# A planned instruction order: the planner's transfer rate set to 360 instead of 400 GB/s

## Chip, cores and metric

The kernel runs on one core of a Trainium2 chip. The metric is the device time of one execution in microseconds (us). A profile gives one execution in detail: its span goes from the first to the last instruction, and its own time is a little longer.

## What is computed

One layer of an encoder: 1024 tokens, width 2048, everything in float32. One input projection (2048 to 6752 columns) feeds two groups of heads, and one output projection joins them.

```python
u = x @ w_in                                    # q, k, v, z, q_idx, k_idx, w_idx, z_ssd, xbc, dt
score = sum_h relu(q_idx[h] @ k_idx.T) * w_idx[h]     # token indexer, 16 heads of 64
sel = top_k(where(chunk(key) <= chunk(query), score, -inf), 256)
o_attn = softmax(rope(q) @ rope(k)[sel].T / sqrt(128)) @ v[sel] * silu(z)   # 8 heads, 2 of k and v
o_ssd = rms_norm(ssd(silu(conv4(xbc)), dt) * silu(z_ssd)) * norm_w          # Mamba-2 mixer
out = layer_norm(2 ** 0.25 * x + concat(o_attn, o_ssd) @ w_out)
```

## The kernel before, in words

**The work.** Each float32 matrix is split into a high and a low part ("xh" and "xl" for inputs, "wh" and "wl" for weights): ACT makes the high part by a rounding copy, DVE or POOL the low part by a subtraction (`t_xst`, line 766; `w_split`, line 916). A product is then three matmuls of 128 x 128 by 128 x 512: high-high, high-low, low-high. The program is a list of pieces made by `units` (line 591). Pieces of the input projection ("T", `emit_t`, line 1163) hold one tile of 128 columns and 512 tokens each; pieces of the output projection ("O", `emit_o`, line 1213) come last. Two groups of tiles are computed as paired products, four small products in phases with sums of weights and of inputs in place of eight plain ones: first k, v and q, later the rest of xbc, zs and z. Sums of weights are made from two or three loads into the "wr" buffers (`t_wacc`, line 880); sums of inputs are made once (`t_xform`), written to scratch in HBM and read back as xfM and xfS. The output projection uses seven products in place of eight; the sums of its weights ("ts") are made long before by `t_wsum` (line 814) and stored.

**What goes on beside it.** Intermediate results go through scratch in HBM and come back: q, k, v, z, the conv outputs (c), the states of the mixer, the mixed output (mx), the halves of the paired products (p). The top-k (`t_topk`, line 1520) is a search by bits: passes of ACT with a sign and a sum, each followed by a few tiny operations on DVE. `s_q` (line 1636) stores a quarter of four heads: the target of one such store has 4 heads by 32 rows by 512. All transfers but the first few are issued by the SP queue.

**What sets the order.** The order of the instructions is not written by hand. While the program is being built, a planner (`Flow`, line 354) runs all tasks as generators beside the list of pieces. Each task says with `Need` what it waits for: free buffers, events, and the engines that it will use. When a task is let go, its instructions are put at the end of each engine's stream at once, and a model of the chip (`Sim`, line 132) moves its clocks: one for PE, DVE ("V"), ACT ("A"), POOL ("G"), the SP queue, and "D", the one lane on which all transfers follow each other. A result gets the time at which the model has it ready.

`ready` (line 432) lets a task go when these times, those of its earlier results and its events, lie before the present by the model, when buffers are free, and when the engines it names are not further ahead than `SLACK` (2600 ns; twice that for tasks of the first priority). Tasks that name "D" (`t_wsum`, `t_form`, `t_pre`, `t_gb`) are held back when the lane of the transfers is too far ahead. `pump` (line 477) lets tasks go in order of priority until the clock of PE has moved on; `await_tiles` (line 505) does so while the operands of the next matmuls are not ready by the model. `w_there` (line 961) looks at the landing of a weight before its split is placed, and `pick` (line 463) chooses DVE or POOL for some operations by the clocks.

On the chip each engine runs its stream in this order and waits by semaphores for what is really needed. The clocks of the model decide nothing there any more: if a transfer lands later than planned, the engine stands at the instruction that needs it, and so does all that is queued behind it.

**The model of a transfer** is `Sim.dma` (line 287): 350 ns of issue on the SP queue, then the bytes on the lane at a rate and 0.6 ns for each row, then `LAND`, 2500 ns, until the result may be used. A transfer also waits for one of 8 places (`lanes`) to come free.

Of the kernel before, what the change touches and what calls it, by code (L numbers as in the profile page):

```python
# [15 lines left out]
D = 2048  # L16
# [107 lines left out]
def in_dram(x):  # L124
    return "DRAM" in str(x.space)
# [6 lines left out]
class Sim:  # L132
# [154 lines left out]
    def dma(self, eng, out, in_, kw):  # L287
        q = {"SP": "SP", "A": "AQ", "G": "G"}[eng]
        lanes = self.lanes["G" if q == "G" else "H"]
        at, notes = self.deps([out], [in_], "D")  # L290
        start = max(self.clk[q], at, lanes.pop(0))
        issue = 1000.0 if eng == "G" else 350.0
        self.clk[q] = start + issue
        sb = in_ if in_dram(out) else out
        row = max(sb.ap[-1][1] * 4, 64)
        x = max(start + issue, self.clk["D"])
        self.clk["D"] = x + max(out.size(), in_.size()) * 4 * (1 / 400 + 0.6 / row)
        cell = [self.clk["D"] + self.LAND, start]
        lanes.append(cell[0])
        self.note(notes, cell, "D")  # L300
        return cell
# [1986 lines left out]
```

## Time and profile before

| what | value |
|---|---|
| runs of the kernel | 1725.16, 1729.61, 1730.37 us (median 1729.61) |
| the profiled execution, own time | 1725.14 us |
| its span | 1723.4 us |
| mean granted clock of TensorE | 0.986 |
| bytes moved by the DMA engines | 446.50 MB, 259 GB/s over the span |

How to read the profile: PE is the matmuls, PEld the loading of their stationary operand, DVE the vector engine, ACT the scalar engine, POOL the general one, SP the queue that issues transfers. A row of a timeline has the start, the duration, the engine, the line, the operation with its output and inputs by name, and in brackets how long the engine stood idle before and what ended that. A window row has the busy time and count of each engine, the granted clock (1.00 is full speed), the mean share of the 16 DMA engines that were busy, and GB/s. All instructions pass through one helper, so that they share a line and are told apart by the names of their tiles.

### The profile page before, as it was taken

To read this page: it belongs to the slowest core of one execution; us is meant where nothing else is said; L and a number is where in the kernel's file an instruction comes from. 1 tells how busy PE (TensorE), PEld (TensorE's weight loads), DVE (VectorE), ACT (ScalarE), POOL (GpSimd) and SP (SyncE) were. 2 spreads that over 40 slices of the span, in tenths; PEclk is the share of its full clock that TensorE was granted. 3 is DMA by queue.
4 is the path that set the end of the run, shared out by engine and by line. 5 is a ranking of instruction groups with operands and counts; after the bars stand their busy time and mean duration, and the time that the engine had idled before them with its cause. 6 is when DMAs were issued, how large, how long until landed. Compare 5 with 4: busy or idle time off the path is not lost. (4 is left out here: it accounts for less than half of the span.)

```text
span 1723.4 us, 24378 instructions
## 1 busy us (share of the span) xinstructions
PE 1638.7 (95%) x8044; PEld 1351.2 (78%) x8044; DVE 1353.0 (79%) x2444; ACT 1019.6 (59%) x1799; POOL 173.5 (10%) x201
## 2 busy tenths in 40 slices
PE   9999999998887989999999999989999999999997
PEld 7877788876666978778888788877888877888875
DVE  5779999787567898789996788845777677659998
ACT  5745575678666856987555478456867544532320
POOL 0000010000000000000222111222121110000110
PEclk9999999999899999999999999999999999999998
DMA  9576578988787678989666875658778999877654
GB/s 320 202 253 230 198 258 290 324 310 307 246 294 259 222 266 271 315 299 318 227 220 219 312 236 188 220 186 251 241 230 280 313 314 342 298 278 268 218 193 147
DMA packets 210215, 446.50 MB, mean 259 GB/s; under 512 B 21928, under 2 KB 61992, under 8 KB 210088
## 3 DMA queue, kind: packets, MB, share of 16 engines
q1 hardware_dynamic: 209656, 444.55, 75.9%
q8 instruction: 63, 1.03, 0.2%
q14 instruction: 64, 0.52, 0.1%
q10 hardware_dynamic: 432, 0.39, 0.1%
HBM read 338.56 MB, written 106.30 MB: 258 GB/s over the span
## 5 line engine op out<-in xcount | busy, mean ns | idle before, releaser
L313 PE MATMUL pj<-xh,wh 128*128 128x512 f32 (+1 forms) x1192 | 470.0, 394 | 25.9 <-ACT wh L313 18.0
L313 PE MATMUL pj<-xh,wl 128*128 128x512 f32 (+1 forms) x1192 | 460.1, 386 | 9.3 <-DVE wl L313 9.1
L313 PE MATMUL pj<-xl,wh 128*128 128x512 f32 (+1 forms) x1192 | 458.8, 385 | 0.1
L313 DVE TENSOR_TENSOR wl<-wr,wh 128x1024 fp32r<-128x1024 f32 (+1 forms) x179 | 213.9, 1197 | 113.2 <-ACT wh L313 112.6
L313 PEld LDWEIGHTS pj<-xh,wh 128*128 128x128 f32 x1192 | 227.1, 191 | 70.7 <-ACT wh L313 20.6
L313 PEld LDWEIGHTS pj<-xh,wl 128*128 128x128 f32 x1192 | 226.5, 190 | 58.8 <-DVE wl L313 14.4
L313 PEld LDWEIGHTS pj<-xl,wh 128*128 128x128 f32 x1192 | 227.3, 191 | 41.2 <-DVE xl L313 1.8
L313 ACT ACTIVATE wh<-wr 128x1024 fp32r<-128x1024 f32 (+1 forms) x185 | 190.6, 1033 | 106.7 <-PE pj L313 67.2
L313 PE MATMUL pj<-xh,s 128*128 128x512 f32 (+1 forms) x688 | 222.1, 385 | 1.8 <-DVE u L313 1.6
L313 PE MATMUL a<-u,u 128*128 128x512 f32 (+3 forms) x746 | 171.7, 351 | 16.4 <-DVE u L313 7.0
L313 PEld LDWEIGHTS a<-u,u 128*128 128x128 f32 x746 | 123.3, 189 | 50.1 <-DVE s L313 10.6
L313 PEld LDWEIGHTS pj<-xh,s 128*128 128x128 f32 x688 | 127.7, 188 | 27.3 <-ACT xh L313 2.3
L313 DVE TENSOR_TENSOR u<-u,u 128x512 f32<-128x512 f32 (+7 forms) x212 | 130.2, 627 | 16.1 <-DMA u<-wo 4.5
L313 ACT ACTIVATE u<-s,sm 128x768 bf16<-128x768 f32 (+7 forms) x132 | 129.6, 982 | 21.3 <-DVE sm L313 19.5
L313 DVE TENSOR_TENSOR wr<-wr,wr 128x1024 f32<-128x1024 f32 (+1 forms) x98 | 121.6, 1243 | 20.5 <-DMA wr<-wt 19.4
L313 ACT ACTIVATE u<-a 128x512 fp32r<-128x512 f32 (+4 forms) x115 | 53.4, 479 | 138.0 <-DVE u L313 66.5
L313 PE MATMUL pj<-xl,s 128*128 128x512 f32 (+1 forms) x344 | 130.8, 380 | 0.8 <-DVE xl L313 0.8
L313 ACT ACTIVATE u<-u 128x512 f32<-128x512 f32 (+4 forms) x165 | 91.9, 566 | 61.5 <-DVE u L313 57.3
L313 ACT ACTIVATE a<-a 128x512 f32<-128x512 f32 (+3 forms) x160 | 76.1, 504 | 70.3 <-PE a L313 69.2
L313 DVE TENSOR_TENSOR s<-wr,s 128x1024 fp32r<-128x1024 f32 (+2 forms) x59 | 70.8, 1200 | 30.7 <-ACT s L313 30.5
L313 DVE TENSOR_TENSOR u<-pj,u 128x512 f32<-128x512 f32 (+2 forms) x94 | 62.4, 664 | 36.7 <-PE pj L313 31.0
L313 PE MATMUL pj<-wh,xh 128*128 128x512 f32 x218 | 87.8, 403 | 1.2 <-DVE u L313 1.2
(253 smaller groups left out, 2678.9 us busy)
## 6 DMA issues: line engine op xcount, KB each, us to landing
wr<-wt SPq DMA_DIRECT2D x228, 512.0 KB, 5.3
u<-u SPq DMA_DIRECT2D x100, 256.0 KB, 5.7
u<-wo SPq DMA_DIRECT2D x79, 256.0 KB, 5.1
wr<-ts SPq DMA_DIRECT2D x32, 512.0 KB, 5.7
ts<-u SPq DMA_DIRECT2D x63, 256.0 KB, 4.3
xr<-xt SPq DMA_DIRECT2D x28, 512.0 KB, 4.9
s<-xt SPq DMA_DIRECT2D x28, 512.0 KB, 6.6
u<-mx SPq DMA_DIRECT2D x49, 256.0 KB, 6.3
```

The source lines that it names most:

```text
L313: f(*args, **kw)
```

## The change

One constant of the model: the rate at which a transfer occupies the lane. The instructions stay what they are; as the planner sees later landings, it may place them in another order.

```diff
@@ -294,7 +294,7 @@
         sb = in_ if in_dram(out) else out
         row = max(sb.ap[-1][1] * 4, 64)
         x = max(start + issue, self.clk["D"])
-        self.clk["D"] = x + max(out.size(), in_.size()) * 4 * (1 / 400 + 0.6 / row)
+        self.clk["D"] = x + max(out.size(), in_.size()) * 4 * (1 / 360 + 0.6 / row)
         cell = [self.clk["D"] + self.LAND, start]
         lanes.append(cell[0])
         self.note(notes, cell, "D")
```

## The prediction

> **What bounds the kernel now.** I read the page first, for the span and the busiest engine.
>
> ```profile
> span 1723.4 us, 24378 instructions
> PE 1638.7 (95%) x8044; PEld 1351.2 (78%) x8044; DVE 1353.0 (79%) x2444; ACT 1019.6 (59%) x1799; POOL 173.5 (10%) x201
> ```
>
> TensorE (PE) is busy for 1638.7 of 1723.4 us, so all other engines together can only move the 84.7 us in which it stands still, and whatever slower clock follows such a stop. A change of order leaves the matmuls alone, so the next question is where those 84.7 us lie. The windows view answers it by stage.
>
> ```profile
> core 0: us, PE busy (x) PEld busy (x) DVE busy (x) ACT busy (x) POOL busy (x), PEclk, DMA share, GB/s
> 400.00:650.00 250.00, 210.54 (x1084) 174.63 (x1085) 190.96 (x390) 174.86 (x310) 5.29 (x4) 0.95 0.76 265
> 425.00:463.00 38.00, 26.18 (x112) 18.82 (x111) 19.34 (x45) 22.89 (x42) 2.48 (x2) 0.89 0.74 248
> 500.00:515.00 15.00, 8.83 (x31) 6.37 (x30) 8.33 (x15) 9.89 (x19) 0.00 (x0) 0.77 0.83 296
> 545.00:570.00 25.00, 15.20 (x99) 14.20 (x98) 15.91 (x30) 16.76 (x27) 0.00 (x0) 0.80 0.64 223
> 650.00:1100.00 450.00, 444.95 (x2237) 370.71 (x2236) 369.36 (x725) 306.55 (x553) 63.53 (x66) 1.00 0.77 260
> 1100.00:1350.00 250.00, 240.83 (x1272) 201.51 (x1271) 167.78 (x339) 163.43 (x303) 46.83 (x63) 0.99 0.73 239
> 1350.00:1450.00 100.00, 96.28 (x517) 78.24 (x516) 67.60 (x122) 47.07 (x91) 10.89 (x8) 1.00 0.98 320
> 1450.00:1712.00 262.00, 257.76 (x1204) 213.22 (x1202) 217.51 (x326) 84.06 (x124) 20.88 (x16) 0.99 0.71 242
> ```
>
> Between 400 and 650 us PE loses 39.5 us (250 - 210.54), nearly half of all its idle time, at a granted clock of 0.95. The 450 us after that lose 5.1 us; from 1350 to 1450 the transfers fill the DMA engines (share 0.98) and PE still loses only 3.7 us. So the stage to look at is 400 to 650, which holds most of the first group of paired products (k, v and q). The timeline of PE has five long stops there.
>
> ```profile
> 430.97 0.79 PE L313 MATMUL pj<-xh,wh 128*128 128x512 f32 x1 [3.52 <-ACT xh L313]
> 437.45 0.69 PE L313 MATMUL pj<-xh,wh 128*128 128x512 f32 x1 [3.26 <-ACT xh L313]
> 461.46 0.80 PE L313 MATMUL pj<-xh,wl 128*128 128x512 f32 x1 [3.55 <-DVE wl L313]
> 508.30 0.80 PE L313 MATMUL pj<-xh,wh 128*128 128x512 f32 x1 [5.79 <-ACT wh L313]
> 558.74 0.58 PE L313 MATMUL pj<-xh,wh 128*128 128x256 f32 x1 [9.09 <-ACT wh L313]
> ```
>
> They add up to 25.2 us. The engine named is only the last link. The same stretches of the timeline for ACT and DVE show the link before it.
>
> ```profile
> 430.28 1.15 ACT L313 ACTIVATE xh<-xr 128x512 fp32r<-128x512 f32 x2 [1.54 <-DMA xr<-xfS]
> 457.66 1.23 DVE L313 TENSOR_TENSOR wr<-wr,wr 128x1024 f32<-128x1024 f32 x1 [3.92 <-DMA wr<-wt]
> 460.18 1.22 DVE L313 TENSOR_TENSOR wl<-wr,wh 128x1024 fp32r<-128x1024 f32 x1
> 504.88 1.15 ACT L313 ACTIVATE xh<-xr 128x512 fp32r<-128x512 f32 x2 [1.60 <-DMA xr<-xt]
> 507.21 1.04 ACT L313 ACTIVATE wh<-wr 128x1024 fp32r<-128x1024 f32 x1
> 555.34 2.41 ACT L313 ACTIVATE xh<-s 128x512 fp32r<-128x512 f32 x4 [3.89 <-DMA s<-xt]
> ```
>
> Four of the five go back to a transfer that had not landed. The one at 461.46 is the clearest: the split "wl", for which PE waits, is queued on DVE behind the sum "wr", and that sum held DVE for 3.92 us until its load arrived. The order was written as if the load would be there. (For the stop at 437.45 no row shows a transfer; ACT had been busy.) These are the places that a planned landing time can reach.
>
> After such a stop matmuls run slower for a while, which the spacing of starts shows:
>
> ```profile
> 432.29 0.63 PE L313 MATMUL pj<-xh,wl 128*128 128x512 f32 x1
> 432.71 0.63 PE L313 MATMUL pj<-xh,wh 128*128 128x512 f32 x1
> 441.73 0.39 PE L313 MATMUL pj<-xl,wh 128*128 128x512 f32 x1
> 441.96 0.39 PE L313 MATMUL pj<-xh,wl 128*128 128x512 f32 x1
> ```
>
> 0.42 us from one to the next at 432 us, 0.23 us at 442 us: half speed. A mean clock c over a window of w us is then 2(1-c)w us at half speed: 8.4 us from 425 to 463, 6.9 us from 500 to 515, 10.0 us from 545 to 570. Half of that is lost where PE was working: 4.2 us for the first three stops (1.4 each), at most 3.4 and 5.0 for the other two, since part of those may lie in the stop itself.
>
> **The change, part by part.** One constant in the planner's model of a transfer goes from 1/400 to 1/360 ns per byte. Nothing is removed or added; every cost comes through order. What the model says of a load of 512 KB in rows of 4 KB can be worked out from the code: 350 issue + 524288/400 + 0.6 x 128 + 2500 = 4.24 us before, 4.38 us after, a shift of 0.146 us; for 256 KB it is 0.073 us. In a queue of such loads the shifts add, and as a transfer also waits for one of eight places, the planned clock of SP slips with them. Against that the trace has:
>
> ```profile
> q1 hardware_dynamic: 209656, 444.55, 75.9%
> wr<-wt SPq DMA_DIRECT2D x228, 512.0 KB, 5.3
> ```
>
> First, landing: 5.3 us in the median, so the model is early by 1.06 us and the change takes back 0.146 of it, 14%. Second, rate: 444.55 MB in 75.9% of 1723.4 us are 340 GB/s while the engines work. The model's lane is busy 444.55 MB/400 = 1111 us plus 0.6 ns for each of 209656 packets (an estimate that takes a packet for a row), 126 us: 1237 us before, 1361 us after, and the measured 1308 us lie between. So the rate as a whole gets no truer, and the landing a little.
>
> What follows is a change of order only where a task's readiness lies within the shift. The planner compares a landing with its clock at each step; a shift of 0.15 us for a lone load and of one or two us in a queue of ten flips some choices, and each flip moves instructions and their transfers on SP, ACT, DVE and PE behind others. A flip is not proportional to the shift: a sum such as the one at 457.66 goes behind the split entirely or not at all. Its price is therefore that of a whole stop, its number is small.
>
> Price of the gain: nothing if no stop is hit. If all five went, 25.2 + 4.2 + 3.4 + 5.0 = 37.8 us. I take the two stops at 430.97 and 461.46, which are short, have a head-of-queue wait on a transfer behind them (1.54 and 3.92 us), and so are nearest to what a shift of one or two us can dissolve: 3.52 + 3.55 + 2 x 1.4 = 9.9 us. What is late next there is the load itself, still 1.06 us later than the old plan has it, under other work on ACT and DVE.
>
> Price of the loss: a stop of the kind at 558.74 made new elsewhere, 9.1 to 14.1 us with its slow clock; I take the middle, 11.6 us, because the share of slow time within the stop can't be read from the rows.
>
> The long stop has a cause that the constant can't reach:
>
> ```profile
> 545.10 1.04 SPq L313 DMA_DIRECT2D s<-xt  x2
> 547.23 1.98 SPq L313 DMA_DIRECT2D q<-u  x2
> ```
>
> ```profile
> L313 SPq DMA_DIRECT2D q<-u x16: 511/530/1359, 395.3 to 555.5; - x16
> ```
>
> ```profile
> DMA  9257987569697997899799865422222222255655
> GB/s 225 89 218 314 396 355 232 191 253 287 246 294 253 300 321 307 362 355 341 321 423 396 355 246 225 191 109 109 109 96 109 109 82 109 114 198 164 210 186 198
> ```
>
> (the last fence is the row of slices for 544 to 556 us, 0.3 us each). From 552 us on, the transfers move 109 GB/s at a share of 0.2, three or four engines of sixteen, while ACT waits for "s<-xt" until 555.34. All 16 stores "q<-u" of the kernel lie between 395.3 and 555.5 us, in the stage with the long stops, and a few engines are still working off something when the others are done. The planner knows one lane only. The Trainium skill, in "DMA: Bandwidth & Descriptors", section "Why a DMA increments its semaphore by 16 and not by 1", says that a transfer runs on the largest number of engines, up to 16, that divides the slowest dimensions of both its sides; that is 4 for a q store, whose target begins with 4 heads. The 109 GB/s agree with it. By that the wait at 558.74 is a matter of which transfers meet, and I leave it in the sum of the forecast.
>
> Two covers to test. The planner holds the preparation of the sums of the output weights back when its lane runs ahead of PE, and a slower lane does so oftener:
>
> ```profile
> L313 SPq DMA_DIRECT2D ts<-u x63: 319/327/1457, 88.8 to 955.3; - x63
> L313 SPq DMA_DIRECT2D wr<-ts x32: 319/320/587, 1370.5 to 1586.5; - x32
> ```
>
> The last is stored at 955.3 us and the first is read at 1370.5 us: 415 us of cover, so this costs nothing. And no wait is added to the program, but a wait that moves forward on an engine holds whatever stands behind it; the stage from 650 to 1100 us, which loses only 5.1 us now, has most to lose by that.
>
> Sum: 1725.14 us (the profiled execution, 1.7 us more than its span) - 9.9 = 1715.2 us. The three runs have a median of 1729.61 us, 4.5 us above the profiled one, and the sum on that footing is 1719.7 us. The runs lie between 1725.16 and 1730.37 us, 0.3% apart, which is about what a measurement of this kernel can tell from no change.
>
> **The rivals.** Slower: the flips put a load of x behind two or more of the few-engine stores. Place: the q products, 400 to 650 us, or a later load of weights. It decides when the stores are issued ahead of the load, not behind it as at 545.10. Price 11.6 us: 1741.2 us. For it: the wait is nearly nine times the model's error for a lone load, so the planner walks into it blind. Against it: where the stores fall is largely fixed by the order of the products, which stays.
>
> No change: the shift of 0.15 us moves only transfers and small operations off the path, or gains and losses cancel. Taking 14% off the 25.2 us gives 3.5 us: 1726.1 us. For it: outside 400 to 650 us PE hardly waits for a load at all. The edit could not do nothing at all, since 124 us more are laid on the lane.
>
> Too cautious: transfers are really faster than 400 GB/s, and the new plan lets consumers wait for loads that are there. In single slices of 2.5 us between 1350 and 1450 us they are at most 414 GB/s:
>
> ```profile
> GB/s 292 288 413 375 263 367 328 201 184 201 372 252 211 320 193 341 403 392 377 392 325 396 396 382 222 269 233 294 222 295 254 366 405 414 397 405 393 237 350 386
> ```
>
> ```profile
> PE pj L313 <- ACT wh L313: 18.0, 4, 9.1
> PE pj L313 <- DVE wl L313: 9.1, 9, 3.6
> PE pj L313 <- ACT xh L313: 6.8, 2, 3.5
> ```
>
> PE's 15 waits for split weights and inputs would each grow by 0.146 us, 2.2 us in all: 1731.8 us, which counts as no change. The "HBM Reference" of the Trainium skill, section "Specifications (TRN2)", sides with this: a core streaming alone gets about 425 GB/s, above the share of 358. The mean of 340 GB/s while busy speaks against it here.
>
> **How the numbers follow.** Faster as forecast 0.40, slower by the new stop 0.34, no change 0.20, too cautious 0.06; the last two together are 0.26 within 0.3%. I put the gain ahead because the landing becomes a little truer and the long stops lie where landing is misjudged; the lead is small because the landing is still 0.91 us early after the correction. The predicted time is 1719.7 us. Its own range goes from one short stop gone (1724.7) to 1705, where the three short stops and the one at 508.30 go (10.3 + 4.2 + 5.8 + 3.4 = 23.7 us, 1705.9). The range over all cases takes that lower end, and upwards it reaches to 1749, between one new long stop with all its bounds (1743.7) and two short ones beside it (1753); what lies beyond on each side I put at one in ten.
>
> **What would show it.** Right: the stops at about 431 and 461 us are gone, clock 1.00 there, PE's idle time from 400 to 650 us near 32 us instead of 39.5, other stages within 3 us, and DVE no longer idle before a "wr" sum that stands ahead of a "wl". Wrong by the rival: a new stop of over 5 us with a few-engine tail before it (about 109 GB/s at a share of 0.2). Wrong altogether: PE's idle time moves in stages that have no transfer behind their waits, 1100 to 1200 us for one; then the order has been dealt anew and landing had no part in it.

## The result, and the profile after

The changed kernel takes 1736.92 us (median of 11 runs, 1733.17 to 1740.63), the kernel before 1725.65 us (11 runs, 1724.15 to 1734.67): 1.0053 times as long, with a 95% interval of 1.0038 to 1.0069. It is slower by 11.3 us by the medians and by 9.1 us by that ratio, which goes by all runs; 9.9 us less were forecast. The profiled execution after took 1733.17 us (span 1731.3 us, 7.9 us more than before).

From the page of the changed kernel, the span, the busy times and the main queue:

```profile
span 1731.3 us, 24300 instructions
PE 1646.8 (95%) x8044; PEld 1358.4 (78%) x8044; DVE 1365.5 (79%) x2445; ACT 1015.3 (59%) x1797; POOL 183.2 (11%) x200
q1 hardware_dynamic: 209656, 444.55, 75.5%
```

The same 8044 matmuls and the same 444.55 MB. What the engines do is nearly the same too: the program has one operation more on DVE and one less on POOL, and ACT loads its function tables 58 times in place of 60. PE now stands still for 1731.3 - 1646.8 = 84.5 us, against 84.7 before: no difference. The whole 7.9 us lies in busy time, 1646.8 against 1638.7, so the same matmuls ran slower. The view of the cores gives the clock, first of the kernel before, then of the changed one:

```profile
core 0: 1723.4 us, clock 0.986
```

```profile
core 0: 1731.3 us, clock 0.981
```

By the reading of the prediction that is 2 x 0.014 x 1723.4 = 48.3 us at half speed before and 2 x 0.019 x 1731.3 = 65.8 us after: 17.5 us more, half of which (8.8 us) is lost work. Within the rounding of the clock it is the 8.1 us of busy time. This holds for these two executions. The 0.986 of the kernel before is as high as the highest of 100 others of it, taken beside the experiments: they have 0.982 on the mean at a span of 1724.7 us, the 11 of the changed kernel 0.980 at 1735.1 us. By the same reading some 4 us of those 10.4 are the slow clock, and the rest would be longer standing, which no view of these executions shows. The windows by stage, after:

```profile
0.00:400.00 400.00, 382.63 (x1687) 306.02 (x1688) 324.63 (x528) 243.90 (x422) 32.23 (x45) 0.98 0.76 261
400.00:650.00 250.00, 225.82 (x1154) 185.88 (x1153) 204.65 (x412) 179.85 (x320) 5.72 (x4) 0.97 0.80 280
650.00:1100.00 450.00, 435.69 (x2199) 365.16 (x2198) 361.74 (x714) 287.65 (x533) 71.35 (x68) 0.98 0.73 245
1100.00:1350.00 250.00, 245.85 (x1303) 206.34 (x1302) 181.28 (x347) 169.06 (x316) 44.90 (x60) 1.00 0.79 264
1350.00:1705.00 355.00, 342.46 (x1647) 283.42 (x1646) 271.11 (x413) 134.85 (x209) 26.09 (x20) 0.99 0.77 261
```

and those of the kernel before that were not shown yet:

```profile
0.00:400.00 400.00, 388.30 (x1736) 312.93 (x1736) 332.44 (x535) 243.66 (x420) 25.12 (x44) 1.00 0.76 266
1350.00:1705.00 355.00, 347.60 (x1693) 286.45 (x1692) 278.22 (x434) 131.13 (x214) 30.79 (x23) 1.00 0.79 267
```

PE's idle time by stage, before to after: 11.7 to 17.4, 39.5 to 24.2, 5.05 to 14.31, 9.2 to 4.2, 7.4 to 12.5 us. The stage of the forecast gained 15.3 us; of the 9.9 us forecast 3.52 + 3.55 = 7.1 were idle time. Three others lost 20.1 us together, and the one from 1100 to 1350 us gained 5.0. The clock went down in three stages and up in two. The counts tell how far PE had come: up to 1350 us the order before had done 1736 + 1084 + 2237 + 1272 = 6329 matmuls, the new one 1687 + 1154 + 2199 + 1303 = 6343. It isn't behind there (a count, since small matmuls lie in other places). From 1350 to 1705 us it does 46 fewer, some 9.4 us at 347.60/1693 = 0.205 us each.

PE's timeline after has eleven stops of 2.2 us or more. Eight of them:

```profile
356.21 0.50 PE L313 MATMUL pj<-xh,wh 128*128 128x512 f32 x1 [2.69 <-ACT wh L313]
369.72 0.80 PE L313 MATMUL pj<-xh,wh 128*128 128x512 f32 x1 [4.59 <-ACT wh L313]
635.76 0.50 PE L313 MATMUL pj<-xh,wh 128*128 128x512 f32 x1 [3.91 <-ACT wh L313]
638.76 0.80 PE L313 MATMUL pj<-xh,wl 128*128 128x512 f32 x1 [2.27 <-DVE wl L313]
716.38 0.80 PE L313 MATMUL pj<-xh,wh 128*128 128x512 f32 x1 [5.54 <-ACT wh L313]
799.27 0.79 PE L313 MATMUL pj<-xh,wh 128*128 128x512 f32 x1 [4.21 <-ACT wh L313]
1504.37 0.79 PE L313 MATMUL pj<-wh,xl 128*128 128x512 f32 x1 [6.62 <-DVE xl L313]
1653.55 0.73 PE L313 MATMUL pj<-s,xh 128*128 128x512 f32 x2 [3.91 <-DVE u L313]
```

None of the five long stops of before between 400 and 650 us is left; between 400 and 630 us none is longer than 2.3 us. Seven of the eight shown are new, and most of these wait for ACT's split of a weight. The one at 1653.55 isn't new: the kernel before has it at 1645.62, with 3.68 us. What the new ones cost in clock is seen in windows around them:

```profile
352.00:378.00 26.00, 18.16 (x63) 13.46 (x62) 20.12 (x43) 18.73 (x37) 1.72 (x1) 0.80 0.89 291
630.00:648.00 18.00, 11.82 (x42) 9.11 (x41) 15.92 (x30) 10.07 (x20) 0.00 (x0) 0.81 0.58 198
712.00:724.00 12.00, 7.58 (x20) 5.57 (x21) 9.03 (x21) 10.75 (x21) 0.00 (x0) 0.72 0.65 216
795.00:806.00 11.00, 6.75 (x21) 5.00 (x21) 6.58 (x12) 9.41 (x20) 1.78 (x2) 0.69 1.02 400
1500.00:1512.00 12.00, 7.63 (x27) 6.21 (x28) 5.50 (x9) 4.16 (x7) 0.00 (x0) 0.72 0.56 208
```

2(1-c)w gives 10.4, 6.8, 6.7, 6.8 and 6.7 us at half speed, 37.4 us in all. Before, the clock was 1.00 in each of these five windows, and the prediction's three windows had 8.4 + 6.9 + 10.0 = 25.3 us. In the changed kernel those three have clocks of 0.96, 1.00 and 0.86, 10.0 us at half speed. So the eight places together went from 25.3 to 47.4 us; the rest of the span has some 4.6 us less, which leaves the 17.5 us more.

What PE waits for at 716.38 isn't a transfer. The sum of the weights was made by DVE at 706.89 to 708.11 us; ACT's timeline shows what it did in the meantime:

```profile
708.75 0.58 ACT L313 ACTIVATE u<-pj 128x512 f32<-128x512 f32 x1
...
710.69 1.03 ACT L313 ACTIVATE u<-s,sm 128x896 bf16<-128x896 f32 x1
...
711.84 1.15 ACT L313 ACTIVATE u<-s,sm 128x1024 bf16<-128x1024 f32 x1
...
715.29 1.99 ACT L313 ACTIVATE wh<-wr 128x1024 fp32r<-128x1024 f32 x2
```

For the seven microseconds after that ACT is busy with hardly a pause, mostly with passes of the top-k ("u<-s,sm", "u<-u,sm"), and the split, whose input lies ready, is queued behind them, two splits at once. While the program is built, `w_there` lets a split go only at the start of a piece and only if its sum has been placed; it refuses for that reason 13 times in the changed order, 2 times in the one before, and the five "ACT wh" stops belong to pieces whose splits it had refused. (Not each refusal makes a stop: seven other refused pieces have none of 2.2 us, and the piece of the stop at 635.76 was refused in the order before too. Nor is ACT busy before each: ahead of the split for 356.21 it stood 5.82 us at an operation that waited for DVE.) Two views show both sides of this, PE's waits and the group of DVE's sums, after:

```profile
PE pj L313 <- ACT wh L313: 26.9, 11, 5.5
PE pj L313 <- DVE wl L313: 11.6, 15, 2.3
PE pj L313 <- DVE xl L313: 7.9, 4, 6.6
```

```profile
L313 DVE TENSOR_TENSOR wr<-wr,wr 128x1024 f32<-128x1024 f32 x98 | 123.4, 1261 | 8.2 <-DMA wr<-wt 7.6
```

DVE stands 7.6 us for the loads of its weight sums. In the kernel before the same group stood 19.4 us:

```profile
L313 DVE TENSOR_TENSOR wr<-wr,wr 128x1024 f32<-128x1024 f32 (+1 forms) x98 | 121.6, 1243 | 20.5 <-DMA wr<-wt 19.4
```

This is what the forecast had a later planned landing do: consumers are placed later and wait less for loads. But PE waits 26.9 us in place of 18.0 for the splits of weights on ACT.

### The profile page after: what moved, and what is told of

The parts are those of the page before. It is cut to its first block, busy times and chain, and to the rows that moved or that the text cites. A ratio compares the mean times of both kernels' runs of the same rounds, so it can differ in the third digit from the quotient of the medians.

```text
span 1731.3 us, 24300 instructions
## 1 busy us (share of the span) xinstructions
PE 1646.8 (95%) x8044; PEld 1358.4 (78%) x8044; DVE 1365.5 (79%) x2445; ACT 1015.3 (59%) x1797; POOL 183.2 (11%) x200
## 3 DMA queue, kind: packets, MB, share of 16 engines
q1 hardware_dynamic: 209656, 444.55, 75.5%
## 5 line engine op out<-in xcount | busy, mean ns | idle before, releaser
L313 PE MATMUL pj<-xh,wh 128*128 128x512 f32 (+1 forms) x1232 | 489.1, 397 | 29.8 <-ACT wh L313 26.9
L313 PE MATMUL pj<-xh,wl 128*128 128x512 f32 (+1 forms) x1232 | 478.7, 389 | 11.8 <-DVE wl L313 11.6
L313 PE MATMUL pj<-xl,wh 128*128 128x512 f32 (+1 forms) x1232 | 475.7, 386 | 0.5 <-DVE xl L313 0.5
L313 PE MATMUL pj<-xh,s 128*128 128x512 f32 (+1 forms) x608 | 196.4, 387 | 0.1
L313 DVE TENSOR_TENSOR u<-u,u 128x512 f32<-128x512 f32 (+5 forms) x214 | 135.7, 647 | 12.6 <-ACT u L313 8.3
L313 ACT ACTIVATE u<-s,sm 128x768 bf16<-128x768 int16 (+7 forms) x132 | 129.7, 983 | 14.9 <-DVE sm L313 13.1
L313 PEld LDWEIGHTS pj<-xh,s 128*128 128x128 f32 x608 | 113.0, 188 | 22.5 <-issue 0.7
L313 DVE TENSOR_TENSOR wr<-wr,wr 128x1024 f32<-128x1024 f32 x98 | 123.4, 1261 | 8.2 <-DMA wr<-wt 7.6
L313 PE MATMUL pj<-wh,xl 128*128 128x512 f32 x218 | 85.8, 394 | 6.6 <-DVE xl L313 6.6
L313 PE MATMUL pj<-s,xh 128*128 128x512 f32 x270 | 86.6, 398 | 3.9 <-DVE u L313 3.9
```

The costliest lines, as they stand in the source:

```text
L313: f(*args, **kw)
```

## The experiments

**Is it the rate, or any change of order?** Theory "rate": 360 makes consumers late, and the loss grows with the distance from 400. Theory "deal": any change of a constant deals the order anew, and the size of the change says nothing. Four other rates:

```diff
-        self.clk["D"] = x + max(out.size(), in_.size()) * 4 * (1 / 360 + 0.6 / row)
+        self.clk["D"] = x + max(out.size(), in_.size()) * 4 * (1 / 396 + 0.6 / row)     # r396; r404: 404, r380: 380, r440: 440
```

> The planner's rate 1 per cent lower (396 instead of 400). Theory A (dose): a lower planned rate makes landings late in the plan, splits of weights are placed later, PE stops; the harm goes with the shift, so a tenth of the change's step gives a tenth of its 10 us, +1 us, no difference that can be measured. Theory B (new deal): any shift of the planned times deals the order anew, and the order at 400 has less idle and slow time than its neighbours; then this is as far from 400 as 360 is, some +5 to +15 us.

> The planner's rate 1 per cent higher (404). Dose: -1 us, no difference. New deal: +5 to +15 us, though the rate went the other way.

> Half the step of the change (380). Dose: half of its loss, about +5 us. New deal: anything from 0 to +15 us, not between 396 and 360 in order.

> The same step the other way (440). Dose: landings are planned earlier, splits are placed earlier, so -5 to 0 us, unless engines then stand at transfers that haven't landed (slower by stops that trace to a DMA). New deal: +5 to +15 us.

Measured against 1726.0 us before: 396 took 1755.86 us (1.0171, interval 1.0148 to 1.0194), 404 took 1738.65 (1.0068, 1.0047 to 1.0089), 380 took 1737.49 (1.0068, 1.0046 to 1.0090), 440 took 1753.24 (1.0163, 1.0143 to 1.0183). A step of 1% downwards costs 29.9 us, one of 10% costs 11.3. No dose can be seen in the whole time; a small one could hide among changes of up to 30 us. Then another constant, the planner's latency from one engine to the next, with the rate left at 400:

```diff
-    LAT = 70.0
+    LAT = 71.0
```

> Before with another constant of the planner, which has nothing to do with transfers, moved by 1 ns: the delay from one engine to another, 71 instead of 70. New deal: slower than before by 5 to 25 us like the neighbours of 400. If the rate itself were the cause: no difference.

Measured: 1744.4 us (1.0088, 1.0071 to 1.0104), 17.6 us more, with a constant that isn't the rate of transfers. The whole time goes by the deal.

In one place, though, the traces of these runs show a dose, and it is the place of the forecast. DVE's standing before sums of weights ("wr") for their loads, and PE's idle time from 400 to 650 us:

| planned rate | DVE waits for loads of "wr" sums, us | PE idle, 400 to 650 us |
|---|---|---|
| 360 | 7.6 | 24.2 |
| 380 | 16.8 | 26.5 |
| 396 | 22.9 | 40.5 |
| 400 | 19.4 | 39.5 |
| 404 | 27.4 | 41.4 |
| 440 | 33.2 | 44.7 |
| 400, latency 71 | 21.3 | 47.7 |

```profile
L313 DVE TENSOR_TENSOR wr<-wr,wr 128x1024 f32<-128x1024 f32 x98 | 120.8, 1236 | 37.8 <-DMA wr<-wt 33.2 <-issue 2.5 <-POOL wl L313 1.1
```

(the row of 440). The lower the planned rate, the less DVE waits for these loads, with 396 a little out of line, and the two lowest rates have the least idle time in this stage. It is one execution each, and the latency alone moved that idle time by 8.2 us, so this suggests an effect of the rate here and doesn't prove it. That the stops at 431 and 461 us are gone shows less: none of 396, 404 and the latency of 71 has them at these times either. For 360 and 380 the loss lies elsewhere. From 650 to 1100 us PE stands 5.1 us in the order before, and 14.3, 15.0, 15.8, 10.5, 10.4 and 6.7 us with 360, 380, 396, 404, 440 and the latency of 71.

**Are the few-engine stores behind the stop at 558.74?** The stores of q and k were cut, so that each part has rows as its slowest dimension; the planner was told of one store as before, so the order of all else stays (of the edit one of the two stores is shown, without the helper that issues the parts).

```diff
-        fl.dma(self.q_sc[h][n // 4][:, 32 * t:32 * t + 32], x)
+        fl.dma_in([(self.q_sc[h][n // 4][r, 32 * t:32 * t + 32], x[32 * r:32 * r + 32]) for r in range(4)],
+                  self.q_sc[h][n // 4][:, 32 * t:32 * t + 32], x)      # k: two parts of 64 rows
```

> The order of before, kept: the planner still counts one store, but each q store is issued as four of 32 rows and each k store as two of 64 rows, so that they use all DMA engines. Theory F (few-engine stores): the stop at 558.74 in before (9.09 us) waits for a load behind stores that run on four engines; it shrinks to under 4 us, others from 430 to 510 us shrink too, and the kernel is 8 to 20 us faster. Rival: the load was late for the sheer amount of transfers or for its late issue; no difference, or some us slower for the added issues on SP.

> The same edit in the order of after. F: the stage 400 to 650 us has lost its long stops there already, so only 0 to 6 us are gained, less than in before's order; the slower plan stays slower by more than 10 us. Rival: as much as in before's order, or nothing in both.

The order before with these stores took 1712.83 us (1726.45 without; 0.9919, 0.9902 to 0.9936), the changed order 1724.35 us (0.9992, 0.9979 to 1.0006), 12.6 us less than with whole stores. Both gain about 13 us, and the 11.5 us between the orders stay: the loss has nothing to do with the stores. The order before with the cut stores is the fastest kernel of the study. Its window and the timeline of PE:

```profile
400.00:650.00 250.00, 222.97 (x1147) 187.27 (x1148) 204.16 (x411) 183.36 (x325) 5.38 (x4) 0.95 0.80 276
```

```profile
436.68 0.80 PE L313 MATMUL pj<-xh,wh 128*128 128x512 f32 x1 [5.71 <-ACT xh L313]
540.72 0.58 PE L313 MATMUL pj<-xh,wh 128*128 128x256 f32 x1 [4.93 <-ACT wh L313]
```

27.0 us of idle time where there were 39.5; the stop of 9.09 us is one of 4.93, those at 461.46 and 508.30 are gone, and the first two are one of 5.71.

**Does ACT's top-k work make the splits late?** ACT's Sign passes of the top-k read 128 columns whatever their size, in either order, planned as if whole.

```diff
-            f(*args, **kw)
+            if op == "activation" and len(args) > 2 and args[2] == AF.Sign:
+                f(args[0][:, 0:128], args[1][:, 0:128], args[2], **kw)
+            else:
+                f(*args, **kw)
```

> The order of before, kept: ACT's passes of the top-k search really read 128 columns only, whatever the planner counts (the search's result is then not that of the reference: a part of the comparison is left out), some 0.3 us each instead of 0.6 to 1.15 us. Theory Q (ACT's queue): before has few stops behind such passes, so it gains 3 to 15 us. Rival (transfers): stops are waits for transfers, gain under 5 us.

> The same edit in the order of after. Q: the new stops at 369.7, 635.8, 716.4 and 799.3 us are splits of weights queued on ACT behind these passes; they go, with their slow clock, 15 to 30 us, and the kernel is no slower than before's order with the same edit. Rival (transfers, or the deal as a whole): it gains as much as before's order does and stays some 10 us slower.

Measured: the order before 1718.76 us (0.9952, 0.9933 to 0.9971), the changed one 1725.39 us (0.9992, 0.9978 to 1.0006). The changed order gains 11.5 us, the other 7.7; the gap goes from 11.3 to 6.6 us by the medians, but by the ratios from 0.53% to 0.40%, and their intervals leave open whether it shrinks at all. Three of the stops stay at their places, shorter (4.59 to 3.12 us near 367, 5.54 to 2.53 near 709, 4.21 to 2.97 near 789), the pair near 632 does not get shorter (3.91 and 2.27 to 3.11 and 3.49), and the one near 1500 stays at 6.58. So this work is part of some of those stops, and not all of the loss.

**Is the loss those five stops?** In the changed order the five pieces multiply by a tile that is always there, and no longer wait for their splits (the kernel leaves out these products of the layer).

```diff
...
+                real = self.fixed[:, 0:1].to_broadcast([P, P]) if i in (50, 51, 97, 109, 121) else w
+                self.nc.tensor.engine.matmul(o, real, x, start=first and p.open and kl == 0, stop=last and p.close and kl == 7,
+                                             skip_group_check=skip)
...
```

> The order of after, kept. At five pieces (50, 51, 97, 109, 121 of the list), the ones whose split the planner put off for a whole piece because their sum of weights wasn't placed yet, PE multiplies by a fixed tile that is always there in place of the split weights (these five products are wrong; all instructions but that operand stay). Theory S (put-off splits): their five stops (2.69, 4.59, 3.91 with 2.27, 5.54, 4.21 us, 23.2 us) go with the slow clock after them, and the kernel is 15 to 30 us faster than after, that is 5 to 20 us faster than before. Rival: PE only meets the next late operand, the stops move to the next piece, gain under 6 us.

> The same five products freed in the order of after, with the q and k stores issued in parts as in a_qsplit. If the two causes are separate, the gains add: some 12 us of the stores and what a_nowait gains. If one hides the other, the sum is less by over 5 us.

The first took 1733.18 us (1.0032, 1.0018 to 1.0046), 3.7 us less than the changed kernel; with the cut stores 1721.39 us (0.9961, 0.9947 to 0.9975), 15.5 us less, about 3.7 + 12.6. The five waits held 20.9 us of standing, and 3.7 us come back; the interval of the ratio overlaps that of the changed kernel (1.0038 to 1.0069), so even these are hardly told from nothing. PE's timeline of the first shows where the rest went:

```profile
369.91 0.50 PE L1183 MATMUL pj<-xh,wh 128*128 128x512 f32 x1 [4.37 <-ACT wh L313]
...
641.50 1.01 PE L313 MATMUL a<-u,u 128*128 128x384 f32 x2 [5.81 <-DVE u L313]
...
804.09 0.97 PE L313 MATMUL a<-c,s 128*128 128x128 f32 x4 [4.05 <-DVE u L313]
1503.38 0.80 PE L313 MATMUL pj<-wh,xl 128*128 128x512 f32 x1 [7.06 <-DVE xl L313]
```

Near 356 and 716 us no stop of 2.2 us is left. At the three other places it moves to the next thing that ACT or DVE has to deliver: the next split at 369.91, other operands made by DVE at 641.50 and 804.09. My theory that the put-off splits cause the loss falls.

**Where along the program does the loss arise?** The rate changes only from a point of the planner's clock on: 400 up to 1100 us and another rate after that, or 360 up to 620 us and 400 after that.

```diff
-        self.clk["D"] = x + max(out.size(), in_.size()) * 4 * (1 / 400 + 0.6 / row)
+        self.clk["D"] = x + max(out.size(), in_.size()) * 4 * (1 / (400 if self.clk["PE"] < 1.1e6 else 360) + 0.6 / row)    # late360; late396, late404, late440
+        self.clk["D"] = x + max(out.size(), in_.size()) * 4 * (1 / (360 if self.clk["PE"] < 6.2e5 else 400) + 0.6 / row)    # early360
```

> 400 until the planner's clock of PE is at 1100 us, 360 from there on: the order is that of before for the first two thirds, and dealt anew behind. New deal: the stops up to some 1150 us are those of before, and the rest differs by -5 to +15 us. Dose (a lower rate is late everywhere): the loss of after from there on, which is its stop at 1504.37 (6.62 us) and its slow clock, +5 to +10 us.

> 360 until the planner's 620 us, 400 from there on: after's first part, with its 15.3 us less idle time from 400 to 650 us, and then a deal that is neither before's nor after's. New deal: +5 to +25 us in all. If each part kept its own worth (after's first, before's second): faster than before by 5 to 10 us.

> As late360, but 440 from the planner's 1100 us on. New deal: slower than before by 5 to 25 us here too, with stops of its own behind some 1150 us. Dose in the last third (a lower rate makes the last group of the mixer late, the stop near 1500 us of after, 380 and late360): no stop there, and -5 to +3 us.

> 404 from 1100 us on. New deal: +5 to +25 us. Dose: no difference, no long stop near 1500 us.

> 396 from 1100 us on. New deal: +5 to +25 us, unrelated in size to late360 (+26 us). Dose: a tenth of late360's loss, under 3 us, and no long stop near 1500 us.

360 at the end alone: 1753.06 us (1.0143, 1.0122 to 1.0164), 26.2 us more than before. 396, 404 and 440 there: 1737.75 (1.0061, 1.0045 to 1.0078), 1730.69 (1.0016, 1.0001 to 1.0031) and 1733.12 us (1.0046, 1.0026 to 1.0066). 360 at the start alone: 1727.57 us, the same as before (1.0001, 0.9987 to 1.0014), and it keeps the gain of the stage from 400 to 650 us (25.5 us idle) and also the new stops at 354, 367, 634 and 714 us. Up to 720 us the kernel before has done 3132 matmuls, this one 3128 and the changed one 3118: by that count the gain of the new first part and its stops about balance. (The level time alone doesn't show it, since the part behind is a new deal as well.) PE's timeline of the kernel with 360 at the end:

```profile
1488.66 0.79 PE L313 MATMUL pj<-wh,xh 128*128 128x512 f32 x1 [5.21 <-ACT xh L313]
1505.84 2.06 PE L313 MATMUL o<-s,u 128*64 128x128 f32 x16 [6.31 <-DVE s L313]
1518.67 1.02 PE L313 MATMUL a<-o,xh 128*128 128x1 f32 x8 [2.68 <-DVE xh L313]
```

Long stops around 1490 to 1510 us are in all three kernels whose rate there is lower by 5% or more (360, 360 at the end, and 380 with 6.46 us at 1504.13), and in none of those with 396, 400, 404 or 440. Three cases suggest that this part goes with the lower rate; they don't show it.

**Is it the stop at 1504.37?** DVE's timeline of the changed kernel shows what the split "xl" is queued behind:

```profile
1502.29 0.69 DVE L313 TENSOR_TENSOR xh<-xh,xl 128x512 f32<-128x512 f32 x1 [3.94 <-DMA xl<-mx]
1503.02 0.69 DVE L313 TENSOR_TENSOR u<-xh,u 128x512 f32<-128x512 f32 x1
1503.63 0.69 DVE L313 TENSOR_TENSOR xl<-u,xh 128x512 fp32r<-128x512 f32 x1
```

It is the pattern of the prediction's stop at 461.46: a sum stands ahead of a split and holds DVE for a load, here of mixed output ("mx") whose last store is issued at 1494.59 us and whose load is issued at 1496.58 us. The split's own input was made at 1497 us. One kernel is the changed order with this split ahead of the two sums and nothing else moved; a second has the cut stores too.

```diff
+            fl.hold = [] if kk == 7 else None
             fl.two(raw, raw, t[1], ALU.add)
             fl.two(t[2], raw, t[2], ALU.subtract)
+            if kk == 7:
+                fl.held, fl.hold = fl.hold, None
...
         fl.two(lo, raw, f32(hi), ALU.subtract)
+        for f, args, kw in fl.held if (n, kk) == (2, 5) else ():
+            f(*args, **kw)
```

The two sums are held back where the planner places them and issued behind the split.

> The changed order with one swap on DVE, all else in place: the split "xl<-u,xh" for which PE stands at 1504.37 us goes ahead of the two sums "xh<-xh,xl" and "u<-xh,u" at 1502.29 us, whose load of the mixed output lands only then. Its own inputs were ready at about 1497 us. Theory L (the loss of the changed order is this one stop): the stop of 6.62 us shrinks to 1 to 2 us, since the next split that PE needs is ready at about 1505 us and PE then comes to it at about 1503; about 5 us of standing and 3.4 us of half clock go, 8 to 9 us in all: about 1728 us, ratio to the order before 1.000 to 1.002. Theory D (the place is one of many, and the wait goes on to the next split): a stop of 4 us or more stays within 5 us of there, gain at most 4 us: 1733 us or more, ratio 1.003 or more.

> The same swap, and the stores of q in four parts of 32 rows and of k in two of 64. Theory L: both gains add, since they lie 950 us apart: 1724.4 - 8.5 = about 1716 us, ratio 0.993 to 0.996, within 4 us of the order before with the same stores (1712.8). Theory D: 1721 us or more, ratio 0.997 or more.

Measured: 1733.09 us (1.0037, 1.0020 to 1.0055), 3.8 us less than the changed kernel, and 1721.39 us with the cut stores (0.9973, 0.9959 to 0.9988), 3.0 us less than without the swap. PE's timeline of the first:

```profile
1500.13 0.50 PE L314 MATMUL pj<-wh,xl 128*128 128x512 f32 x1 [1.26 <-DVE xl L314]
...
1513.07 1.25 PE L314 MATMUL a<-o,u 128*128 128x1 f32 x8 [3.46 <-DVE u L314]
```

The stop shrinks from 6.62 to 1.26 us as theory L has it, but some ten microseconds later PE stands 3.46 us for a result of DVE ("u"). In DVE's timeline this result is queued behind a split of a weight that waits for ACT:

```profile
1511.09 1.23 DVE L314 TENSOR_TENSOR wl<-wr,wh 128x1024 fp32r<-128x1024 f32 x1 [1.64 <-ACT wh L314]
1512.23 0.69 DVE L314 TENSOR_TENSOR u<-u,u 128x512 f32<-128x512 f32 x1
```

It comes at 1512.23 us, where the changed kernel has it at 1512.73: PE is there sooner, the result hardly. Theory L gave 8 to 9 us and fell; theory D's time came out, though its place was further on than it said. Each removal, this one and the five waits, takes back a third of the loss at most, by intervals that overlap that of the changed kernel; whether the two add was not run.

**What stays open.** Ten of the eleven other orders that were timed are slower than the one planned with 400, by 3.8 to 29.9 us; the eleventh (360 at the start alone) is level; none is faster. That a change of constant makes a new deal is shown; that the rate acts in the stage of the forecast is likely. Why the deal at 400 stands and slows less than its neighbours elsewhere is not, nor what made the changed order's mixer late at 1500 us, and no removal gave back most of the loss.

## Why the prediction was wrong, step by step

- **The gain** was right in place, and its cause fits: DVE's waits before weight sums fell from 19.4 to 7.6 us and go with the planned rate over six rates, but for one. It was too small: the stage gained 15.3 us of idle time instead of 7.1. The clock, expected at 1.00, was 0.96 from 425 to 463 us.
- **The long stop at 558.74**: its cause was right in part. With the cut stores 4.93 of its 9.09 us are left, and the kernel gains 13.6 us. That the constant can't reach it was wrong; in the new order the stop isn't there. That the transfers meet differently is the likely reason, which no run shows.
- **The size of the shift** was wrong. That "the model is early by 1.06 us" sets the model's 4.24 us for a lone load against a median of 5.3 us of loads that stand in a queue, which the planner counts too. While the program is built, the planner's own times from issue to landing of these 512 KB loads have a median of 5.28 us at 400, as measured, and of 6.32 us at 360. So in the middle the planned landing was not early, and the change moved it about 1 us past the measured one: "the landing becomes a little truer" doesn't hold.
- **The step that failed** is "Its price is therefore that of a whole stop, its number is small." The number isn't small: from the first flip on the planner's clocks differ, and everything behind is dealt anew, as the latency moved by 1 ns showed with 17.6 us. The first half isn't borne out either: five waits of 20.9 us gave back 3.7. The forecast needed "other stages within 3 us", and idle time moved by 5.7, 9.3, -5.0 and 5.1 us in them. Five stops over 3 us went, and five others over 3 us came (369.72, 635.76, 716.38, 799.27 and 1504.37). The measured time lies within the range of the forecast, but on the other side of the kernel before. The chances should have been those of a new order drawn beside a good one, not those of a correction.
- **The price of a stop.** The slow clock was counted for the stops let go and for one new long stop, but no new short stop was expected. In the two profiled executions idle time came out even, 84.7 and 84.5 us, and the loss is the slow clock, 8.8 us by the reading of the cores against 7.9 us of span; over all executions it is some 4 us of 10.4. The Trainium skill, in "TensorE: Matmul & The Clock Gate", Part 1, tells of a clock that halves after an idle window of about 3.4 us; the 10.4 us at half speed behind two stops of 2.69 and 4.59 us agree with three such windows.
- **The rival for slower** had nearly the right size, 11.6 us against 11.3, and the wrong mechanism: the few-engine stores cost both orders the same, and the new stops that were followed back are queues on ACT and DVE, at 1504.37 behind a load of mixed output. The last q or k store of the changed kernel is issued at 547.1 us, and four of its five new stops over 3 us come after that. The agreement is luck.
- **"Too cautious"**: planning faster than 400 loses as well (404 and 440), and DVE then waits longer for loads (27.4 and 33.2 us), so it was no matter of caution either.
- **The cover that I named** was the right one. The stage from 650 to 1100 us "has most to lose" by instructions that hold others behind them; it lost 9.3 us, with the split at 716.38 behind ACT's top-k. My test for "wrong altogether", idle time that moves in stages without a transfer behind their waits, is what happened there; yet it wasn't the whole, as landing did play its part between 400 and 650 us.

## What to carry to other kernels

Where a planner writes the order, any change of one of its constants is first of all another order: time neighbours of the constant, and an unrelated one, before the constant itself is given the credit or the blame. Price a stop with the slow clock behind it, and don't expect its whole length back when its cause is removed, as another wait can take over. What can be mended with the order left as it is, here the shape of two stores, gained more than any constant did.

## What the runs showed of the hardware

- Stores whose slowest dimension is 4 or 2 held up other transfers. The same bytes in parts with 32 or 64 rows in front gained 13.6 us in 20 stores (16 of q, 4 of k), although 52 more transfers were issued on SP, and the stop of 9.09 us shrank to 4.93.
- A stop of 2.3 us can bring slow time. Before the change PE stands 2.29 us at 113.47, and 2.47 us at 1146.80 with 0.77 us more after one matmul, and the clock in the windows around is below 1 without a longer stop in them:

```profile
105.00:140.00 35.00, 31.10 (x135) 24.41 (x134) 31.48 (x56) 16.79 (x33) 0.00 (x0) 0.95 0.54 191
1140.00:1155.00 15.00, 11.42 (x66) 9.85 (x64) 6.12 (x9) 5.30 (x12) 6.07 (x3) 0.89 0.43 157
```

2 x 0.05 x 35 = 3.5 us and 2 x 0.11 x 15 = 3.3 us at half speed; the single stops of 4.2 to 6.6 us above brought 6.7 to 6.8 us. It need not: around the 2.36 us at 586.16 before (580 to 600 us) and the 2.21 us at 518.90 after (514 to 530 us) the clock is 1.00. The length agrees with the window of about 3.4 us on the page of the Trainium skill named above, one for the first two and two for the longer ones; that the standing has to last as long as a window does not, since at 113.47 two thirds of it were enough.
